# Even and odd tokens as the two streams of every product, and prompt attention over eight key blocks per head

## The chip, the core and the metric

The kernel runs on one core of a Trainium2 chip. Five engines work side by side: TensorE (PE; its weight loads are listed apart as PEld), VectorE (DVE), ScalarE (ACT), GpSimd (POOL) and SyncE (SP), which here only issues transfers. Each engine takes its instructions in the order that the scheduler wrote, and waits for others through semaphores. The metric is device microseconds of one execution, median of several; less is better.

## What is computed

One layer of a decoder, for a prompt of 256 tokens and for 8 sequences of 4 new tokens each (288 tokens in all), with 2048 features. Cut to what matters:

```python
z = x @ w_in                                  # h, gate_b, gate_c, q, k, v, g_a, g_b
ya = gate_b * causal_conv3(gate_c * h)
for g, (window, dil) in enumerate(((128, 1), (512, 4), (2048, 16))):   # 4 heads of 128 each
    # key s is allowed for query t if (t - s) % dil == 0 and 0 <= t - s <= 128 * dil
    score[g] = q[g] @ k[g].T / sqrt(128) - slope * (t - s)
yb = merge over g of softmax(score[g]) @ v[g]  # weights: the softmax denominators
x1 = LN1(ALPHA * x + (sigmoid(g_a) * (ya @ w_a) + sigmoid(g_b) * (yb @ w_b)) @ w_out)
a, b = x1 @ w_up
y = LN2(ALPHA * x1 + (silu(causal_conv3(a)) * b) @ w_down)
```

The new tokens attend to caches of keys and values; the caches are copied to outputs too. Merging the groups by their denominators is one softmax over the keys of all three groups.

## The kernel before

Everything is held by feature: 128 features on the partitions, tokens along the free dimension. The unit of work is a **product** (lines 186 to 212): one block of 128 output features for all 288 tokens. Its weight block of up to 16 x 128 x 128 comes by one transfer of up to 1 MB on SP's queue (`prepare`, three buffers "wst"), and is split into a rounded part and a rest ("whi" on ScalarE, "wlo" on VectorE, line 136 on, in half blocks, four buffers each). The activations are split the same way (`split`, line 213). `mms` then runs three matmuls for each of the 16 blocks of features, lines 208 to 210: high by high, low weight or low activation by high.

The moving operand of a matmul is read from two streams. The free dimension of x is stored as [2, 144 or more], "h" and "a", and the matmul takes column (a, h): one element of the first half, one of the second. PSUM tiles ("acc", five buffers) are [a, h]. Before, stream 0 holds tokens 0 to 143 and stream 1 tokens 144 to 287, so SBUF is in the order of the tokens and PSUM interleaves them; `h2`, `h3`, `pieces` and `from_psum` are the views that undo this.

`prompt_attention(j, ...)` (line 320) is a generator that is stepped by the products, so that its rows of matmuls stand between them; `in_a_row` keeps a row together, behind the last product matmul. For each of four heads j it takes all three groups at once. Two blocks of 128 queries (qb) see one and two blocks of 128 keys: scores (line 326), addition of the distance penalty from a table m_dist (line 332), softmax (337 to 341), transposes of V (346) and of the probabilities (354), and the value matmuls (362). A group's 128-key block is a unit here: three for the first query block, six for the second, nine for a head. Keys that the dilation rules out are in the table with a distance of 1e30. The PSUM tiles of this part are "att" (two buffers) and some of "acc".

`sample_steps` (line 407) is a second generator for the new tokens: matmuls against cache tiles, each of them 32 columns of the array wide (lines 421 and 474, PSUM tile "long", one buffer), and two small rows for the new keys and values (lines 438 and 485).

After attention come the mixer products with the convolution (`conv_in`, `conv`, `gated`, lines 524 to 563), the output products with the first norm, and the feed-forward part in three thirds of 16, 16 and 12 blocks: up products in pairs with convolution and gate, then 16 down products. In the first third the norm is applied to the products' results (`normed`, line 731), and the normed x is split for the later thirds in the down loop (line 781). In the last third the subtraction of a mean estimate n2.c (line 785, GpSimd) and the sums of the second norm (`Norm.add`, lines 639 and 640, GpSimd) run along. `finish_out` (line 671) ends the kernel: norm, gain and bias (lines 706 and 708), and six output transfers.

The tile framework's scheduler simulates the engines and orders each engine's instructions by it; `behind(i, after)` (line 118) pins one instruction behind another, without a wait.

## Time and profile before

| what | us |
|---|---|
| median of 3 runs (lowest, highest) | 1762.09 (1761.49, 1762.12) |
| profiled execution | 1763.11 |
| its span | 1761.3 |
| VectorE busy in it | 1008.2 |
| ScalarE busy in it | 798.4 |
| GpSimd busy in it | 254.8 |

How to read the profile's lines. A row of the timeline has the start and duration in us, the engine, the line of the kernel, the operation, output and inputs, the shapes, and how many instructions are merged (x10: ten of them in that stretch). A bracket gives the idle time of the engine before it and what ended that. A row of a grouped view ends with busy us, mean ns of one, and idle time before. A row of a view by stretches gives the stretch, its length, busy us with the number of instructions for PE, PEld, DVE, ACT and POOL, the granted clock, the DMA share and GB/s. Matmuls overlap in the array, so their spacing, not their duration, is what one costs. A matmul on 32-bit operands (not split) shows as two records.

### The profile page before, as it was taken

The numbers are of one execution on the slowest core, as the hardware profiler recorded it, in microseconds if no ns is written. First come the engines' busy times: TensorE is split into PE (matmuls) and PEld (weight loads), VectorE is DVE, ScalarE is ACT, GpSimd is POOL, SyncE is SP. The second block draws the span as 40 slices with busy tenths as digits, with TensorE's granted clock in tenths as the row PEclk, the third lists the DMA queues.
The fourth block names the chain that finished last, engine by engine and source line by source line (L and its number), as shares of the span: only waits on it lengthen the run. The fifth ranks groups of instructions, "written<-read, shape, count | busy, mean of one in ns | idle before, by whom it ended". The sixth has DMA issues, their size and how long they took to land.

```text
span 1761.3 us, 33600 instructions
## 1 busy us (share of the span) xinstructions
PE 1743.9 (99%) x14269; PEld 1714.4 (97%) x14269; DVE 1008.2 (57%) x1322; ACT 798.4 (45%) x1174; POOL 254.8 (14%) x403
## 2 busy tenths in 40 slices
PE   9999999999999999999999999999999999999996
PEld 9999999999999999999999999999999999999996
DVE  5444455545555444455588888774555554555554
ACT  5444444333434333344445656553454443345444
POOL 0000000000000000001155233310011110011174
PEclk9999999999999999999999999999999999999998
DMA  8477787787787887466766566656565656666662
GB/s 325 173 288 264 271 299 297 265 324 297 271 333 285 304 312 269 150 241 252 269 259 220 210 241 226 229 219 236 219 236 219 236 217 238 217 238 217 223 212 105
DMA packets 60919, 436.25 MB, mean 248 GB/s; under 512 B 7265, under 2 KB 8929, under 8 KB 16865
## 3 DMA queue, kind: packets, MB, share of 16 engines
q1 hardware_dynamic: 59040, 429.40, 65.9%
q10 hardware_dynamic: 1728, 4.72, 0.7%
q8 instruction: 111, 1.82, 0.4%
q14 instruction: 40, 0.32, 0.0%
HBM read 389.89 MB, written 94.53 MB: 275 GB/s over the span
## 4 chain that ended last, share of the span: by engine, by line
PE 96%; POOL 1%; ACT 1%; DVE 1%; issue 0%; DMA 0%; ACTq 0%; DVEq 0%
PE acc L208 31%; PE acc L210 31%; PE acc L209 31%; PE acc L276 1%; PE long L421 1%; PE long L474 1%; POOL dd L785 1%; PE att L362 0%; PE att L326 0%; ACT whi L138 0%; POOL qk_s L549 0%; ACT xh L214 0%; ACT yah L708 0%; DVE dd L684 0%; DMA yah<-in_x 0%
## 5 line engine op out<-in xcount | busy, mean ns | idle before, releaser
L139 DVE TENSOR_TENSOR wlo<-wst,whi 128x1024 fp32r<-128x1024 f32 (+1 forms) x578 | 706.9, 1224 | 617.3 <-ACT whi L138 613.2
L138 ACT CAST whi<-wst 128x1024 fp32r<-128x1024 f32 (+1 forms) x578 | 590.0, 1022 | 871.2 <-PE acc L209 767.7
L208 PE MATMUL acc<-xh,whi 128*128 128x288 f32 (+1 forms) x3216 | 923.0, 287 | 0.0
L210 PE MATMUL acc<-xh,wlo 128*128 128x288 f32 (+1 forms) x3216 | 920.5, 286 | 0.0
L209 PE MATMUL acc<-xl,whi 128*128 128x288 f32 (+1 forms) x3216 | 920.4, 286 | 0.0
L208 PEld LDWEIGHTS acc<-xh,whi 128*128 128x128 f32 x3216 | 607.8, 189 | 7.9 <-ACT h L569 2.5
L210 PEld LDWEIGHTS acc<-xh,wlo 128*128 128x128 f32 x3216 | 607.8, 189 | 0.8 <-issue 0.8
L209 PEld LDWEIGHTS acc<-xl,whi 128*128 128x128 f32 x3216 | 607.9, 189 | 0.3 <-issue 0.2
L208 PE MATMUL acc<-yah,whi 128*128 128x288 f32 x1216 | 348.0, 286 | 0.3 <-ACT yah L214 0.3
L210 PE MATMUL acc<-yah,wlo 128*128 128x288 f32 x1216 | 347.7, 286 | 0.6 <-DVE wlo L139 0.6
L209 PE MATMUL acc<-yal,whi 128*128 128x288 f32 x1216 | 347.6, 286 | 0.0
L208 PEld LDWEIGHTS acc<-yah,whi 128*128 128x128 f32 x1216 | 229.7, 189 | 3.1 <-ACT h L591 2.5
L210 PEld LDWEIGHTS acc<-yah,wlo 128*128 128x128 f32 x1216 | 229.8, 189 | 0.8 <-DVE wlo L139 0.8
L209 PEld LDWEIGHTS acc<-yal,whi 128*128 128x128 f32 x1216 | 229.8, 189 | 0.0
L549 POOL COPY qk_s<-u 128x2 f32<-128x2 f32 x44 | 41.5, 943 | 565.7 <-ACT u L758 441.1
L535 DVE SCALAR_TENSOR_TENSOR cy<-u,prm,cy 128x304 f32<-128x304 f32 x120 | 71.1, 593 | 3.4 <-ACT cy L533 0.7
L606 POOL TENSOR_TENSOR ya<-ya,dd 128x288 f32<-128x288 f32 x16 | 13.6, 851 | 306.0 <-DVE ya L605 306.0
L560 DVE TENSOR_TENSOR ya<-cy,acc 128x144 f32<-128x144 f32 x132 | 25.6, 250 | 33.6 <-PE acc L210 33.6
L549 POOL COPY cm<-u 128x2 f32<-128x2 f32 x16 | 3.0, 185 | 254.3 <-DVE u L574 254.3
L214 ACT CAST yah<-ya 128x288 fp32r<-128x288 f32 x76 | 32.7, 430 | 13.8 <-POOL ya L606 8.3
L214 DVE TENSOR_TENSOR yal<-ya,yah 128x288 fp32r<-128x288 f32 x76 | 34.9, 460 | 1.3 <-ACT yah L214 1.2
L639 POOL TENSOR_TENSOR cache<-cache,dd 128x288 f32<-128x288 f32 x29 | 28.0, 964 | 49.0 <-DVE dd L724 33.5
(179 smaller groups left out, 852.8 us busy)
## 6 DMA issues: line engine op xcount, KB each, us to landing
wst<-in_w_in SPq DMA_DIRECT2D x113, 1024.0 KB, 6.0
wst<-in_w_up SPq DMA_DIRECT2D x88, 1024.0 KB, 4.8
wst<-in_w_down SPq DMA_DIRECT2D x32, 1024.0 KB, 4.8
cache<-in_ck SPq DMA_DIRECT2D x18, 1024.0 KB, 6.4
out_o_ck<-cache SPq DMA_DIRECT2D x18, 1024.0 KB, 9.1
cache<-in_cv SPq DMA_DIRECT2D x18, 1024.0 KB, 6.3
out_o_cv<-cache SPq DMA_DIRECT2D x18, 1024.0 KB, 9.8
wst<-in_w_a SPq DMA_DIRECT2D x16, 1024.0 KB, 4.8
```

Of the source, the lines that this page charges most:

```text
L138: act.copy(hi[:, :n, :], st[:, k0 : k0 + n, :])
L139: dve.tensor_tensor(lo[:, :n, :], st[:, k0 : k0 + n, :], f32(hi[:, :n, :]), ALU.subtract)
L208: pe.matmul(out, hi[:, c, :], xh_k, start=k == 0, stop=False)
L209: pe.matmul(out, hi[:, c, :], xl_k, start=False, stop=False)
L210: last_mm[0] = pe.matmul(out, lo[:, c, :], xh_k, start=False, stop=k == nk - 1)
L214: return act.copy(hi, src), dve.tensor_tensor(lo, src, f32(hi), ALU.subtract)
L276: i = pe.matmul(o[b], first_w(term == 2, b, k), xk, start=k == 0 and term == 0, stop=k == KD - 1 and term == 2)
L421: row.append(pe.matmul(p[j * NS : (j + 1) * NS], qm[:, j, b, :], c[:, o + j * cols : o + (j + 1) * cols], start=b == 0, stop=b == NB - 1,))
L535: dve.scalar_tensor_tensor(y, u[:, i : i + YW], prm[:, w0 + i : w0 + i + 1], y, ALU.mult, ALU.add)
L549: pool.tensor_copy(dst[:, 0:2], u[:, SEQ : SEQ + 2])
L560: dve.tensor_tensor(a, b, c, ALU.mult)
L639: pool.tensor_tensor(self.s1, self.s1, d, ALU.add)
```

## The change

The two streams of a product are now the even and the odd tokens: stream h, column a is token 2a + h. PSUM is then in the order of the tokens, and SBUF tiles by feature hold evens first and odds behind, except K, V, the convolution's input and the final y, which are stored in the order of the tokens. The views change with it: x is split from a stepped view at the start, convolution input and gates go by `of_tokens` and `of_halves`, and y is written with a step of two.

In prompt attention the two query blocks are the even and the odd queries. In the groups with dilation 4 and 16 an even query sees even keys only, and an odd query odd keys, so one block of 128 keys (taken with a step of two) is enough for each; the group with dilation 1 needs both blocks of 128 keys for either. That makes four blocks for each of the two, eight for a head. The table m_dist is loaded by parity of the rows, with four transfers and a memset; the transposed probabilities go to two "acc" tiles of 512 columns.

Further, the two small rows of the new tokens are attached to the last row of their group (the first of them with an "att" tile in place of "long"). In the first third's down loop the split of the normed x is pinned behind the last gated split and the latest weight split; in the last third the subtraction of n2.c for block i is pinned behind the sums of block i - 3.

```diff
+MW = (2 + NG - 1) * P
...
+    def t2(ap):
+
+        return ap.rearrange("p (a h) -> p h a", h=2)
...
+    w_split = []
+
     def half_block(st, k0, n):
         hi = sb(wp, [P, HK, P], "whi", F32R, bufs=4)
         lo = sb(wp, [P, HK, P], "wlo", F32R, bufs=4)
-        act.copy(hi[:, :n, :], st[:, k0 : k0 + n, :])
-        dve.tensor_tensor(lo[:, :n, :], st[:, k0 : k0 + n, :], f32(hi[:, :n, :]), ALU.subtract)
+        w_split[:] = split(hi[:, :n, :], lo[:, :n, :], st[:, k0 : k0 + n, :])
         return hi, lo, n
...
     for k0, n, _ in FIRST:
         k = slice(k0, k0 + n)
-        splits.append(split(xh[:, k, :, :H], xl[:, k, :, :H], h3(xs[:, k])))
+        splits.append(split(xh[:, k, :, :H], xl[:, k, :, :H], xs[:, k].rearrange("p k (a h) -> p k h a", h=2)))
...
-    m_dist = pa[:, : C_W - C_M0]
-    pa_at = [C_W - C_M0]
+
+    m_dist = pa[:, : 2 * NG * SEQ].rearrange("p (h g k) -> p h g k", h=2, g=NG)
+    pa_at = [2 * NG * SEQ]
...
-    s_two = [pa_take(NG * 2 * P) for _ in range(2)]
+    s_two = [pa_take(MW) for _ in range(2)]
...
-    sT_flat = [xs_flat[:, NH * NG * T + c * NG * P : NH * NG * T + (c + 1) * NG * P] for c in range(3)]
-    sT_three = [t.rearrange("p (g q) -> p g q", g=NG) for t in sT_flat]
+    sT_two = [xs_flat[:, NH * NG * T + c * MW : NH * NG * T + (c + 1) * MW] for c in range(2)]
...
+    def load_distances():
+
+        pool.memset(m_dist[: P // 2, :, :, P:], BIG)
+        m0, m1 = (
+            ins["cst"][:, c : c + NG * n * P].rearrange("(a h) (g k) -> h a g k", h=2, g=NG)
+            for n, c in ((1, C_M0), (2, C_M1))
+        )
+        for h in range(2):
+            behind(sp.dma_start(m_dist[: P // 2, h, :, :P], m0[h]), w_load[0])
+            behind(sp.dma_start(m_dist[P // 2 :, h], m1[h]), w_load[0])
...
     def prompt_attention(j, qT, kT, vT):
 
-        blocks = [(qb, g, P * (qb + 1)) for qb in range(2) for g in range(NG)]
-        s3 = att(NG * P), att(2 * 2 * P), sb(ps, [P, 2 * P], "acc")
-        p_at = [(s3[0], g * P) for g in range(NG)] + [(s3[1], 0), (s3[1], 2 * P), (s3[2], 0)]
-        in_a_row([last_mm[0]] + [
-            pe.matmul(t[:, c : c + nk], qT[:, g, qb * P : (qb + 1) * P], kT[:, g, :nk], start=True, stop=True)
-            for (t, c), (qb, g, nk) in zip(p_at, blocks)
-        ])
-        s = [s_two[qb][:, : NG * P * (qb + 1)].rearrange("p (g k) -> p g k", g=NG) for qb in range(2)]
-        for (t, c), (qb, g, nk) in zip(p_at, blocks):
-            c0 = qb * NG * P + g * nk
-            dve.scalar_tensor_tensor(
-                s[qb][:, g, :], m_dist[:, c0 : c0 + nk], -SLOPE[g][j] / SCALE, t[:, c : c + nk], ALU.mult, ALU.add
-            )
+
+        q4 = h3(qT)[:, :, :, :P]
+        k4, v4 = (t[:, :, :SEQ].rearrange("p g (a h) -> p g h a", h=2) for t in (kT, vT))
+        s3 = [att(MW) for _ in range(2)]
+        row = [last_mm[0]]
+        for qb in range(2):
+            row += [
+                pe.matmul(s3[qb][:, : 2 * P], q4[:, 0, qb], kT[:, 0, :SEQ], start=True, stop=True)
+            ] + [
+                pe.matmul(s3[qb][:, (1 + g) * P : (2 + g) * P], q4[:, g, qb], k4[:, g, qb], start=True, stop=True)
+                for g in range(1, NG)
+            ]
+        in_a_row(row)
+        s = s_two
+        for qb in range(2):
+            for g in range(NG):
+                c, n = (0, 2 * P) if g == 0 else ((1 + g) * P, P)
+                m = m_dist[:, qb, g] if g == 0 else t2(m_dist[:, qb, g])[:, qb]
+                dve.scalar_tensor_tensor(
+                    s[qb][:, c : c + n], m, -SLOPE[g][j] / SCALE, s3[qb][:, c : c + n], ALU.mult, ALU.add
+                )
...
         pv = [att(NG * P) for _ in range(2)]
         row = [last_mm[0]] + [
-            pe.transpose(pv[kb][:, g * P : (g + 1) * P], vT[:, g, kb * P : (kb + 1) * P], ident)
+            pe.transpose(
+                pv[kb][:, g * P : (g + 1) * P], vT[:, 0, kb * P : (kb + 1) * P] if g == 0 else v4[:, g, kb], ident
+            )
             for kb in range(2) for g in range(NG)
         ]
         for kb in range(2):
             act.copy(v[:, kb], pv[kb].rearrange("p (g d) -> p g d", g=NG))
-        pairs = ((0, 0), (1, 0), (1, 1))
-        pt = [att(NG * P), att(NG * P), sb(ps, [P, NG * P], "acc")]
+        pt = [sb(ps, [P, MW], "acc") for _ in range(2)]
         in_a_row(row + [
-            pe.transpose(t[:, g * P : (g + 1) * P], s[qb][:, g, kb * P : (kb + 1) * P], ident)
-            for t, (qb, kb) in zip(pt, pairs) for g in range(NG)
+            pe.transpose(pt[qb][:, c * P : (c + 1) * P], s[qb][:, c * P : (c + 1) * P], ident)
+            for qb in range(2) for c in range(MW // P)
         ])
-        for sT, t in zip(sT_three, pt):
-            act.copy(sT, t.rearrange("p (g q) -> p g q", g=NG))
+        for sT, t in zip(sT_two, pt):
+            act.copy(sT, t)
...
         po = att(2 * P)
         in_a_row([last_mm[0]] + [
             pe.matmul(
-                po[:, qb * P : (qb + 1) * P], v[:, kb, g], sT[:, g],
-                start=kb == 0 and g == 0, stop=kb == qb and g == NG - 1,
+                po[:, qb * P : (qb + 1) * P], v[:, c if c < 2 else qb, max(0, c - 1)], sT_two[qb][:, c * P : (c + 1) * P],
+                start=c == 0, stop=c == MW // P - 1,
             )
-            for sT, (qb, kb) in zip(sT_three, pairs) for g in range(NG)
+            for qb in range(2) for c in range(MW // P)
         ])
         act.copy(oT, po)
-        split(ybh[:, j, :SEQ], ybl[:, j, :SEQ], oT)
+        split(h2(ybh[:, j])[:, :, :P], h2(ybl[:, j])[:, :, :P], oT.rearrange("p (h a) -> p h a", h=2))
...
+                if g == NG - 1 and b == NB - 1:
+
+                    pn = att(NG * NS)
+                    row += [
+                        pe.matmul(
+                            pn[j * NS : (j + 1) * NS, k * NS : (k + 1) * NS], q_s[:, k, j, :], k_s[:, k, j, :],
+                            start=True, stop=True,
+                        )
+                        for k in range(NG) for j in range(NH)
+                    ]
...
-        pn = sb(ps, [P, NG * NS], "long", bufs=1)
-        for j in range(NH):
-            for g in range(NG):
-                pe.matmul(
-                    pn[j * NS : (j + 1) * NS, g * NS : (g + 1) * NS], q_s[:, g, j, :], k_s[:, g, j, :],
-                    start=True, stop=True,
-                )
...
+                if g == 0 and b == NB - 1:
+
+                    row += [
+                        pe.matmul(
+                            p[j * NS : (j + 1) * NS], sTn[:, j * NS : (j + 1) * NS], vn[:, j, :], start=False, stop=True
+                        )
+                        for j in range(NH)
+                    ]
...
-                for j in range(NH):
-                    pe.matmul(
-                        p[j * NS : (j + 1) * NS], sTn[:, j * NS : (j + 1) * NS], vn[:, j, :], start=False, stop=True
-                    )
...
-            if j == 1:
-                dst, src = ((cst, ins["cst"][:, :C_M0]), (m_dist, ins["cst"][:, C_M0:]), (prm, ins["prm"]))[g]
-                behind(sp.dma_start(dst, src), w_load[0])
-        pool.tensor_copy(q_s[:, :, j, :], q_all[:, j, :, SEQ:])
+            if j == 1 and g == 1:
+                load_distances()
+            elif j == 1:
+                behind(sp.dma_start(*((prm, ins["prm"]) if g else (cst, ins["cst"][:, :C_M0]))), w_load[0])
+        pool.tensor_copy(q_s[:, :, j, :].rearrange("p g (a h) -> p g h a", h=2), h3(q_all[:, j])[:, :, :, P:])
     steps_on[0] = True
     for j in range(NH):
         kT, vT = (kv[:, j % 2, c] for c in range(2))
         for g in range(NG):
             for t in (kT, vT):
-                act.copy(h2(t[:, g, :]), product(x))
+                act.copy(t[:, g, :].rearrange("p (a h) -> p a h", h=2), product(x).rearrange("p h a -> p a h"))
...
-    def samples(t):
-        return t[:, SEQ:].rearrange("p (b r) -> p b r", b=NB)
-
-    def pieces(up, us):
-
-        return up[:, :H], up[:, H:SEQ], us
-
-    def from_psum(o):
-        return o[:, 0], o[:, 1, : SEQ - H], o[:, 1, SEQ - H :].rearrange("p (b r) -> p b r", b=NB)
+    def of_tokens(p, s):
+
+        return t2(p), s.rearrange("p b (r h) -> p h b r", h=2)
+
+    def of_halves(t):
+
+        return t[:, :, :P], t[:, :, P:].rearrange("p h (b r) -> p h b r", b=NB)
 
     def last_rows(dst, u):
         pool.tensor_copy(dst[:, 0:2], u[:, SEQ : SEQ + 2])
@@ -555,12 +590,14 @@
     def gated(out, y, o, add=None):
 
         yt = y[:, SEQ : SEQ + NB * (NT + 2)].rearrange("p (b r) -> p b r", b=NB)
-        if add is None:
-            for a, b, c in zip(pieces(out, samples(out)), pieces(y, yt[:, :, 2:]), from_psum(o)):
+        for a, b, c in zip(of_halves(h2(out)), of_tokens(y[:, :SEQ], yt[:, :, 2:]), of_halves(o)):
+            if add is None:
                 dve.tensor_tensor(a, b, c, ALU.mult)
-        else:
-            for a, b, c in ((out[:, :SEQ], y[:, :SEQ], o[:, :SEQ]), (samples(out), yt[:, :, 2:], samples(o))):
+            elif len(a.shape) == 3:
                 dve.scalar_tensor_tensor(a, c, add, b, ALU.add, ALU.mult)
+            else:
+                for h in range(2):
+                    dve.scalar_tensor_tensor(a[:, h], c[:, h], add, b[:, h], ALU.add, ALU.mult)
...
-                            dve.tensor_scalar(y[:, i], dd[:, i], self.at(self.g, i), self.at(self.b, i), ALU.mult, ALU.add)
+                            dve.tensor_scalar(t2(y[:, i]), h2(dd[:, i]), self.at(self.g, i), self.at(self.b, i), ALU.mult, ALU.add)
                     else:
-                        act.activation(y[:, i], dd[:, i], AF.Identity, bias=self.at(self.b, i), scale=self.at(self.g, i))
+                        act.activation(t2(y[:, i]), h2(dd[:, i]), AF.Identity, bias=self.at(self.b, i), scale=self.at(self.g, i))
...
                 pa, b1 = normed(pa)
-                act.activation(up, pa[:, :SEQ], AF.Identity, bias=b1)
-                act.activation(us, samples(pa), AF.Identity, bias=b1)
+                for a, b in zip(of_tokens(up, us), of_halves(pa)):
+                    act.activation(a, b, AF.Identity, bias=b1)
             else:
-                for a, b in zip(pieces(up, us), from_psum(pa)):
+                for a, b in zip(of_tokens(up, us), of_halves(pa)):
                     act.copy(a, b)
...
-            split(gh[:, k], gl[:, k], gf)
+            last_split = split(gh[:, k], gl[:, k], gf)
...
             if part == 0:
-                split(x[0][:, i], x[1][:, i], h2(dd[:, i]))
+                for i_x, *before in zip(split(x[0][:, i], x[1][:, i], h2(dd[:, i])), last_split, w_split):
+                    for b in before:
+                        behind(i_x, b)
                 dve.scalar_tensor_tensor(h2(dd[:, i]), h2(dd[:, i]), ALPHA, o, ALU.mult, ALU.add)
             else:
                 if f == KF and i > 0:
-                    pool.tensor_tensor(dd[:, i], dd[:, i], n2.c, ALU.subtract)
+                    i_c = pool.tensor_tensor(dd[:, i], dd[:, i], n2.c, ALU.subtract)
+                    if i > 2:
+                        behind(i_c, sums[i - 3])
                 dve.tensor_tensor(h2(dd[:, i]), h2(dd[:, i]), o, ALU.add)
             if f == KF:
                 if i == 0:
                     n2.first()
-                n2.add(i)
+                sums.append(n2.add(i))
```

More of the change, by code (lines that the diff above doesn't have):

```diff
@@ L320, in prompt_attention @@
     def prompt_attention(j, qT, kT, vT):
[L322 to L334 removed]
+        q4 = h3(qT)[:, :, :, :P]
[18 more added lines that the diff above has]
+                )
         for qb in range(2):
             st = sb(wk, [P, 4], "st", bufs=4)
[L337 removed]
+            dve.reduce_max(st[:, 0:1], s[qb], AX.X)
             dve.tensor_scalar_mul(st[:, 1:2], st[:, 0:1], -SCALE)
@@ L494, in sample_steps @@
         act.copy(oT, po)
-        split(ybh[:, :, SEQ:], ybl[:, :, SEQ:], oT.rearrange("p (j r) -> p j r", j=NH))
+        split(*(h3(t)[:, :, :, P:] for t in (ybh, ybl)), oT.rearrange("p (j a h) -> p j h a", j=NH, h=2))
         yield
@@ L572, in layer_kernel @@
         up, us = conv_in(u[:, :UW], R_SM + i * 2 * NB)
-        for a, b, c in zip(pieces(up, us), pieces(h, samples(h)), from_psum(pc)):
+        for a, b, c in zip(of_tokens(up, us), of_halves(h2(h)), of_halves(pc)):
             dve.tensor_tensor(a, b, c, ALU.mult)
@@ L635, in add @@
             act.activation(q, d, AF.Square)
+            i_sum = None
             if i == 0:
-                pool.tensor_copy(self.s1, d)
+                i_sum = pool.tensor_copy(self.s1, d)
             elif not last or not self.tail:
                 pool.tensor_tensor(self.s1, self.s1, d, ALU.add)
-                pool.tensor_tensor(self.s2, self.s2, q, ALU.add)
+                i_sum = pool.tensor_tensor(self.s2, self.s2, q, ALU.add)
             if i == KD - 2:
@@ L654, in add @@
                         pe.matmul((self.p1, self.p2)[k % 2], ones_d, w[:, k], start=k < 2, stop=k >= 2)
+            return i_sum
         def at(self, c, i):
@@ L738, in normed @@
         dve.scalar_tensor_tensor(t, n1.nmr, w[:, 0:1], t, ALU.mult, ALU.add)
-        return t, w[:, 1:2]
+        return h2(t), w[:, 1:2]
     cf = sb(big, [P, KF, 2 + 2 * NB], "qk_s")
@@ L744, in layer_kernel @@
     n2 = Norm(R_LN + 2 * KD, R_LN + 3 * KD, True)
+    sums = []
     for part, nf in enumerate(THIRDS):
```

1 line of the change is left out of this document (removed).

## The prediction

> **What bounds the kernel now.** I read the page first: the engines' busy time and the chain that ended last.
>
> ```profile
> span 1761.3 us, 33600 instructions
> PE 1743.9 (99%) x14269; PEld 1714.4 (97%) x14269; DVE 1008.2 (57%) x1322; ACT 798.4 (45%) x1174; POOL 254.8 (14%) x403
> PE 96%; POOL 1%; ACT 1%; DVE 1%; issue 0%; DMA 0%; ACTq 0%; DVEq 0%
> ```
>
> TensorE is busy for 1743.9 of 1761.3 us and carries 96% of the chain. So only three things can move the end: fewer or shorter TensorE instructions, the few gaps between them, and the two ends of the span where TensorE does not run. Everything that the other engines gain or lose counts only if it reaches one of these. The second view is what TensorE waited for, in us, times and longest.
>
> ```profile
> PE acc L226 <- DVE cy L223: 1.2, 1, 1.2
> PE acc L210 <- DVE wlo L139: 0.6, 1, 0.6
> PE acc L208 <- ACT yah L214: 0.3, 1, 0.3
> PE acc L276 <- ACT yal L214: 0.2, 1, 0.2
> ```
>
> That is 2.3 us in all, 1.4 of it at the start. The idle time of 17.4 us is therefore mostly the tail, about 15 us after the last matmul. The third view gives busy time in two stretches: the first third of the up-projection, the densest for VectorE, and the later feed-forward work.
>
> ```profile
> 900.00:1100.00 200.00, 200.00 (x1627) 200.00 (x1626) 163.60 (x206) 114.28 (x187) 83.18 (x100) 1.00 0.63 229
> 1500.00:1700.00 200.00, 200.00 (x1635) 200.00 (x1634) 112.27 (x154) 91.58 (x148) 36.13 (x62) 1.00 0.63 229
> ```
>
> From the second row, 200 us over 1635 matmuls, one product matmul takes 0.1223 us; two of them are 0.245 us. In the first row VectorE (third figure) is busy 163.6 of 200 us, ScalarE 114.3, GpSimd 83.2. Even there TensorE is never short of work.
>
> **The products.** Each product issues the same matmuls, with the same operand shapes: a column still takes one element of the first stored half and one of the second. Only the token that stands there differs. Main cost: nothing added, nothing removed.
>
> **Prompt attention, scores.** Before, a head has three 128-wide and three 256-wide score matmuls; after, four 128-wide and two 256-wide. Each shows as two records.
>
> ```profile
> 114.36 0.29 PE L210 MATMUL acc<-xh,wlo 128*128 128x288 f32 x1
> 114.48 1.70 PE L326 MATMUL att<-dd,yah 128*128 128x128 f32 x10
> 116.02 0.59 PE L326 MATMUL acc<-dd,yah 128*128 128x256 f32 x2
> 116.57 0.29 PE L209 MATMUL acc<-xl,whi 128*128 128x288 f32 x1
> ```
>
> From the last product matmul before the row to the second one behind it, 116.57 - 114.36 = 2.21 us; less two product matmuls, the 12 records cost 1.965 us. The row of value matmuls of the same head gives the price of a narrow record:
>
> ```profile
> 138.12 0.29 PE L210 MATMUL acc<-xh,wlo 128*128 128x288 f32 x1
> 138.24 2.17 PE L362 MATMUL att<-yah,yal 128*128 128x128 f32 x18
> 140.37 0.29 PE L209 MATMUL acc<-xl,whi 128*128 128x288 f32 x1
> ```
>
> 140.37 - 138.12 - 0.245 = 2.005 us over 18 records, 0.1114 each. Six narrow score records are then 0.668 us, and a wide one is (1.965 - 0.668)/6 = 0.216. After: 8 x 0.1114 + 4 x 0.216 = 1.755 us, so 0.21 less for a head, **0.84** for four.
>
> **Value matmuls.** Nine per head become eight: two records less, 4 x 2 x 0.1114 = **0.89** us.
>
> **Transposes of the probabilities.** Nine per head become eight.
>
> ```profile
> 174.22 0.64 PEld L354 LDWEIGHTS att<-cst,yal 128*128 128x128 f32 x6 [0.84 <-ACT yal L350]
> ```
>
> Six loads in 0.64 us, 0.107 each; four fewer are **0.42** us. The six transposes of V stay. Attention saves 2.15 us together.
>
> The unknown here is the operand step. For the second and third head group the keys are now read with a step of two elements (16 matmuls, 32 records), and V for its transposes too. The trace before has no such step on TensorE. Its nearest rows are the product matmuls, whose columns alternate between two places 640 or 576 bytes apart and still take only 0.1223 us for 288 columns. From below the cost is nothing; from above I double a narrow record, 32 x 0.1114 = 3.6 us. I take nothing, as the nearest row jumps further and pays nothing.
>
> The Trainium skill (SBUF — State Buffer, "Door 1: The DMA port swizzle", note on cachelines) says that an access which crosses to a new 16-byte line pays unless two accesses hit the line. A step of two fp32 elements has exactly two hits, so by the rule the step is free and the sum is unchanged; but the products, with one hit on each line in turn, should by the same rule run slow, and the rows above do not bear that out.
>
> **Places of the rows.** The transposed probabilities now use two accumulator buffers, not two attention buffers and an accumulator, so they no longer wait for V's copies. In the first head that wait let sample work in between:
>
> ```profile
> 130.82 0.31 PEld L354 LDWEIGHTS att<-cst,yal 128*128 128x128 f32 x3 [0.20 <-issue]
> 131.30 0.15 PEld L421 LDWEIGHTS long<-cache,sw 128*32 128x32 f32 x6 [0.17 <-issue]
> ```
>
> Each change between the two shapes cost 0.17 to 0.20 us of weight-load idle; two of them may go. I take 0.2 us (bounds 0 and 0.4). The two small sample rows (new keys' scores, new values) are attached to the last row of their group, where before they broke into a product:
>
> ```profile
> 443.73 0.29 PE L210 MATMUL acc<-xh,wlo 128*128 128x288 f32 x1
> 443.94 0.65 PE L438 MATMUL long<-qk_s 128*32 128x32 f32 x24
> 444.74 0.29 PE L209 MATMUL acc<-xl,whi 128*128 128x288 f32 x1
> ```
>
> 444.74 - 443.73 - 0.245 = 0.77 us, of which the 24 records, issued over about 0.46 us, remain; 0.25 to 0.3 us is the break. I take 0.25 for each of the two rows, **0.5** us (bounds 0 and 0.6). The new keys' scores move from the single "long" buffer to an attention buffer, so they need not wait for VectorE to empty the former; prompt attention, whose second head stands at 174 us, has released its buffers by 443.
>
> **The two gaps in the middle.** The first lies at the end of the first third:
>
> ```profile
> 1166.81 0.29 PE L209 MATMUL acc<-yal,whi 128*128 128x288 f32 x1
> 1167.44 0.51 PE L208 MATMUL acc<-yah,whi 128*128 128x288 f32 x2 [0.34 <-ACT yah L214]
> ```
>
> 1167.44 - 1166.81 - 0.122 = 0.51 us. Behind it:
>
> ```profile
> 1155.23 4.42 POOL L549 COPY qk_s<-u 128x2 f32<-128x2 f32 x1 [9.71 <-ACT u L754]
> ```
>
> ```profile
> 1155.44 3.03 DVE L214 TENSOR_TENSOR xl<-dd,xh 128x288 fp32r<-128x288 f32 x8
> ```
>
> Eight VectorE splits of the next x in a row, drawn ahead of the last gated block, held a two-element GpSimd copy for 4.42 us, and the block's chain came late. The change puts each of those splits behind the last gated split and behind the latest weight split. The 16 pairs then stand in the down products, where both engines idle at each weight split. The second gap:
>
> ```profile
> 1703.74 0.29 PE L209 MATMUL acc<-yal,whi 128*128 128x288 f32 x1
> 1704.62 0.39 PE L210 MATMUL acc<-yah,wlo 128*128 128x288 f32 x1 [0.60 <-DVE wlo L139]
> ```
>
> 1704.62 - 1703.74 - 0.122 = 0.76 us. Its cause:
>
> ```profile
> 1681.88 15.96 POOL L785 TENSOR_TENSOR dd<-dd,cache 128x288 f32<-128x288 f32 x14 [13.56 <-ACT cache L628]
> ```
>
> ```profile
> 1699.75 0.44 ACT L635 ACTIVATE cy<-dd 128x288 f32<-128x288 f32 x1 [4.25 <-POOL cache L640]
> ```
>
> ```profile
> 1702.67 1.90 DVE L139 TENSOR_TENSOR wlo<-wst,whi 128x1024 fp32r<-128x1024 f32 x1 [5.48 <-ACT whi L138]
> ```
>
> Fourteen GpSimd subtractions issued in a row delayed the sums, ScalarE waited 4.25 us for a buffer, its weight cast came late and VectorE's with it. The change holds subtraction i behind sum i - 3. I count both gaps as gone: **1.27** us. What is late next is the same chain with a shorter head; TensorE already waits for nothing else there.
>
> **Other engines.** Convolution input and gate go from three instructions (144, 112, 32 wide) to two (256, 32) in mixer and later thirds, which saves fixed cost off the path. In the first third the gate goes from two instructions to three, about 0.2 us for each of 16 blocks, against 36 us of VectorE slack in 200: hidden. Should it not be hidden it is 3 us. PSUM rows read with a step of two cost nothing on ScalarE, as these two copies show, the first stepped and the second not:
>
> ```profile
> L515 ACT COPY dd<-acc 128x288 f32<-128x288 f32 x24 | 9.4, 392 | 0.0
> L628 ACT COPY cache<-att 128x288 f32<-128x288 f32 x2 | 0.8, 395 | 0.3 <-PE att L627 0.3
> ```
>
> 392 against 395 ns. A step of two in SBUF I have only by that neighbour. The distance table takes four transfers instead of one, plus a memset on GpSimd: about three more issues on SP's queue, some 1.5 us, ahead of the next weight load on the same queue. Three weight buffers and a split block stand ahead of TensorE, each a product long (48 x 0.1223 = 5.9 us). Hidden; if the cover fails, 1 to 2 us.
>
> **The ends.** At the start x is split from a stepped view:
>
> ```profile
> 4.87 0.67 ACT L214 CAST xh<-yah 128x576 fp32r<-128x576 f32 x1 [0.94 <-DMA yah<-in_x]
> 6.12 0.85 PE L276 MATMUL acc<-xh,yal 128*128 128x288 f32 x2 [0.21 <-ACT yal L214]
> ```
>
> TensorE starts on the first casts. If a stepped read costs twice, the first x cast adds 0.67 us and VectorE's split as much: 0 to 1.3 us. I take 0.1. In the tail, ScalarE and VectorE now write y with a step:
>
> ```profile
> 1752.32 4.77 ACT L708 ACTIVATE yah<-dd,prm 128x288 f32<-128x288 f32 x9 [0.39 <-DVE dd L684]
> 1754.98 1.44 DVE L706 TENSOR_SCALAR yah<-dd,prm 128x288 f32<-128x288 f32 x4
> ```
>
> Nine ScalarE rows end at 1757.09, four VectorE rows at 1756.42, and output transfers follow. Bounds: nothing, or a doubling, +4.8 us on ScalarE. I take 0.3 us.
>
> **Sum.** -0.84 - 0.89 - 0.42 - 0.2 - 0.5 - 1.27 + 0.1 + 0.3 = -3.7 us. The profiled execution took 1763.11 us with its span of 1761.3 (1.8 around it), 1.0 above the median of 1762.09. So a span of about 1757.6, an execution of 1759.4, and a median of **1758.4 us**, 0.21% faster. A difference of 0.2% (3.5 us) is about what a measurement of this kernel can tell from no change, so the sum sits on that line.
>
> **Rivals.** First, *new gaps take part of it back*. The scheduler orders every engine anew, and the first third has VectorE at 82% with an instruction added in each block. For it: two such gaps of 0.5 and 0.8 us stand in the kernel before, both from other engines' order. Against it: the change pins the orders behind exactly these. If the two gaps stay or two others of 0.5 to 0.8 come, and the row breaks bring nothing, the sum is -3.7 + 1.27 + 0.7 = -1.7: 1760.4 us, within 0.2%.
>
> Second, *the step of two costs double wherever it stands on the path*: 3.6 us in attention's score records, 4.8 in the tail's ScalarE rows, 1.3 at the start, 9.7 together. Then +6.0 us, **1768.1 us**, slower. It decides from +7.2 us, so it needs attention and most of the tail. For it: no row shows a stepped SBUF access on these engines. Against it: stepped PSUM reads at 392 ns and the alternating product operand.
>
> Third, *the change does less than it says*: attention's 2.15 us only. That comes if TensorE's gaps and breaks are set by something else: 1760.3 us with the ends as taken, again within 0.2%.
>
> **Chances.** Forecast 0.50 (faster by over 0.2%), first and third rivals together 0.36 (within), second 0.14 (slower). Range: below, everything open comes free (-0.4 at the ends), the row breaks come at their upper bounds (-0.3), and each of eight other sample rows loses a break of 0.25 us too (2.0), 1755.6 with rounding; above, the second rival with half its price, 1763.3, and a little more for its upper part: 1755.6 to 1765.
>
> **What would show it.** Right: the score, value and transpose rows shorter by 0.21, 0.22 and 0.1 us a head, with a narrow stepped record at 0.11; no TensorE wait above 0.3 us near the end of the first third and in the last 60 us; y's ScalarE rows still 0.53 us apart. Wrong: stepped records at 0.2, ScalarE's tail rows near 1 us, a later first matmul, or new waits of TensorE for a weight split. A time above 1763 would say that a stall was made, not that the savings are missing.

## The result, and the profile after

The changed kernel takes 1757.22 us (median of 10 runs, 1756.95 to 1758.0) against 1761.66 (10 runs, 1761.42 to 1762.37): 4.4 us less, ratio 0.9975 with a 95% interval of 0.9967 to 0.9982. The prediction was 1758.4, 3.7 us less. The page of the changed kernel:

```profile
span 1756.2 us, 33518 instructions
PE 1738.8 (99%) x14257; PEld 1710.7 (97%) x14257; DVE 1006.7 (57%) x1278; ACT 797.9 (45%) x1142; POOL 243.7 (14%) x404
...
PE 99%; DMA 0%; DVE 0%; ACT 0%; SPq 0%; ACTq 0%; issue 0%; DVEq 0%
```

TensorE now carries 99% of the chain, against 96%. What TensorE waited for in the changed kernel:

```profile
PE acc L235 <- DVE cy L232: 1.2, 1, 1.2
PE acc L285 <- ACT yal L223: 0.7, 2, 0.4
PE acc L285 <- ACT whi L223: 0.3, 1, 0.3
```

Only waits at the start are left; the two gaps of the middle (0.6 on a weight split and 0.3 on a gated split) are gone. The two stretches shown of before:

```profile
900.00:1100.00 200.00, 200.00 (x1627) 200.00 (x1626) 165.10 (x217) 113.31 (x186) 79.41 (x98) 1.00 0.63 226
1500.00:1700.00 200.00, 200.00 (x1635) 200.00 (x1634) 113.53 (x144) 94.33 (x140) 36.92 (x63) 1.00 0.64 229
```

The first third is not lighter for VectorE (163.6 before), and the pace of a product matmul is the same, 200 us over 1635. So the gain is not in the products. It is in the rows between them and in the two gaps. The first head's scores, from the last product matmul to the second one behind the row:

```profile
113.72 0.29 PE L219 MATMUL acc<-xh,wlo 128*128 128x288 f32 x1
113.84 0.59 PE L349 MATMUL att<-dd,yah 128*128 128x256 f32 x2
114.28 0.62 PE L351 MATMUL att<-dd,yah 128*128 128x128 f32 x4
...
115.74 0.29 PE L218 MATMUL acc<-xl,whi 128*128 128x288 f32 x1
```

115.74 - 113.72 - 0.245 = 1.775 us, against 1.965 before: 0.19 less. The four narrow records read keys with a step of two, and stand (0.62 - 0.276)/3 = 0.115 us apart. The value row:

```profile
134.71 0.29 PE L219 MATMUL acc<-xh,wlo 128*128 128x288 f32 x1
134.83 1.95 PE L391 MATMUL att<-yah,yal 128*128 128x128 f32 x16
...
136.74 0.29 PE L218 MATMUL acc<-xl,whi 128*128 128x288 f32 x1
```

136.74 - 134.71 - 0.245 = 1.785 us, 0.22 less than 2.005. V's and the probabilities' transposes now stand in one block:

```profile
127.25 0.29 PE L219 MATMUL acc<-xh,wlo 128*128 128x288 f32 x1
127.27 0.78 PEld L374 LDWEIGHTS att<-cst,dd 128*128 128x128 f32 x6
127.38 0.86 PE L374 MATMUL att<-cst,dd 128*128 128x128 f32 x6
128.07 1.04 PE L383 MATMUL acc<-cst,yal 128*128 128x128 f32 x8
...
129.07 0.29 PE L218 MATMUL acc<-xl,whi 128*128 128x288 f32 x1
```

129.07 - 127.25 - 0.245 = 1.575 us for all fourteen, with no wait for V's copies. The row of sample work that stood among them in the first head before has moved to 142 us, where it costs 2.08 us by itself. Before, both together took 4.15 us (128.09 to 132.48, less two product matmuls), so the first head's transposes gain 0.50 us. In the other heads there is next to nothing to gain; the second one, before and after:

```profile
171.49 0.29 PE L210 MATMUL acc<-xh,wlo 128*128 128x288 f32 x1
...
175.38 0.29 PE L209 MATMUL acc<-xl,whi 128*128 128x288 f32 x1
```

```profile
169.75 0.29 PE L219 MATMUL acc<-xh,wlo 128*128 128x288 f32 x1
...
171.56 0.29 PE L218 MATMUL acc<-xl,whi 128*128 128x288 f32 x1
```

175.38 - 171.49 - 0.245 = 3.645 us before, with a sample row of 2.05 among it, so 1.595; 171.56 - 169.75 - 0.245 = 1.565 after: 0.03 less. Further on, a sample row by itself, and the last one of the keys, which now has the new keys' scores behind it:

```profile
346.50 0.29 PE L219 MATMUL acc<-xh,wlo 128*128 128x288 f32 x1
346.71 1.92 PE L450 MATMUL long<-cache,sw 128*32 128x512 f32 x16
...
348.79 0.29 PE L218 MATMUL acc<-xl,whi 128*128 128x288 f32 x1
```

```profile
409.40 0.29 PE L219 MATMUL acc<-xh,wlo 128*128 128x288 f32 x1
409.62 1.92 PE L450 MATMUL long<-cache,sw 128*32 128x512 f32 x16
411.36 0.37 PE L458 MATMUL att<-qk_s 128*32 128x32 f32 x24
...
411.88 0.29 PE L218 MATMUL acc<-xl,whi 128*128 128x288 f32 x1
```

Alone, a row costs 348.79 - 346.50 - 0.245 = 2.05 us; with the new keys' scores 411.88 - 409.40 - 0.245 = 2.24. They cost 0.19 us, against 0.77 where they broke into a product. GpSimd's two-element copy near the end of the first third, 4.42 us before:

```profile
1149.44 0.79 POOL L584 COPY qk_s<-u 128x2 f32<-128x2 f32 x1 [7.69 <-ACT u L795]
```

The tail rows of y, now written with a step of two (ScalarE's):

```profile
1747.04 4.83 ACT L747 ACTIVATE yah<-dd,prm 128x288 f32<-128x288 f32 x9 [0.35 <-DVE dd L723]
```

4.83 us for nine against 4.77.

**The start must be taken out before profiles are compared.** The spans differ by 5.1 us, 0.7 more than the medians. In the profiled execution of before, TensorE ran the first product matmuls at half pace until 10.7 us (the first row: two of them in 0.69 us, 0.24 apart; the second, at full pace: two in 0.41, 0.12 apart):

```profile
7.33 0.69 PE L276 MATMUL acc<-xh,yal 128*128 128x288 f32 x2
...
10.85 0.41 PE L276 MATMUL acc<-xh,yal 128*128 128x288 f32 x2
```

In the changed kernel full pace was there with the first product matmuls, at 6.35 us: the first two took 0.51 us behind a wait, where the profiled execution of before took 0.85 at 6.12. Its first x cast took 0.72 us where before it took 0.67:

```profile
5.05 0.72 ACT L223 CAST xh<-yah 128x576 fp32r<-128x576 f32 x1 [1.12 <-DMA yah<-in_x]
...
6.35 0.51 PE L285 MATMUL acc<-xh,yal 128*128 128x288 f32 x2 [0.44 <-ACT yal L223]
```

So I measure from the last of the first three products (last start of their low-weight records) to the norm's matmuls behind the last product. The view of one line has the first and the last start. Before:

```profile
L276 PE MATMUL acc<-xh,wlo x16: 286/286/447, 10.0 to 26.2; 128*128 128x288 f32 x16
```

```profile
L648 PE MATMUL att<-cache,ones_d x4: 406/406/406, 1744.2 to 1744.9; 128*128 128x288 f32 x4
```

1744.2 - 26.2 = 1718.0 us. After:

```profile
L285 PE MATMUL acc<-xh,wlo x16: 286/286/286, 8.7 to 25.5; 128*128 128x288 f32 x16
```

```profile
L686 PE MATMUL att<-cache,ones_d x4: 406/406/406, 1738.9 to 1739.6; 128*128 128x288 f32 x4
```

1738.9 - 25.5 = 1713.4 us, 4.6 us less. The tail behind it is 1761.3 - 1744.2 = 17.1 us before and 1756.2 - 1738.9 = 17.3 after.

### The profile page after: what moved, and what is told of

The parts are those of the page before. It is cut to its first block, busy times and chain, and to the rows that moved or that the text cites. A ratio compares the mean times of both kernels' runs of the same rounds, so it can differ in the third digit from the quotient of the medians.

```text
span 1756.2 us, 33518 instructions
## 1 busy us (share of the span) xinstructions
PE 1738.8 (99%) x14257; PEld 1710.7 (97%) x14257; DVE 1006.7 (57%) x1278; ACT 797.9 (45%) x1142; POOL 243.7 (14%) x404
## 4 chain that ended last, share of the span: by engine, by line
PE 99%; DMA 0%; DVE 0%; ACT 0%; SPq 0%; ACTq 0%; issue 0%; DVEq 0%
PE acc L217 32%; PE acc L219 31%; PE acc L218 31%; PE long L506 1%; PE long L450 1%; PE acc L285 1%; DMA dd<-in_w_in 0%; PE att L391 0%; ACT yah L747 0%; DVE dd L723 0%; PE att L351 0%; PE acc L383 0%; PE att L349 0%; PE att L374 0%; PE att L687 0%; PE att L686 0%
## 5 line engine op out<-in xcount | busy, mean ns | idle before, releaser
L223 DVE TENSOR_TENSOR wlo<-wst,whi 128x1024 fp32r<-128x1024 f32 (+2 forms) x584 | 709.1, 1215 | 613.1 <-ACT whi L223 607.6
L223 ACT CAST whi<-wst 128x1024 fp32r<-128x1024 f32 (+2 forms) x584 | 593.3, 1017 | 888.0 <-PE acc L218 777.7
L595 DVE TENSOR_TENSOR ya<-cy,acc 128x256 f32<-128x256 f32 x88 | 23.5, 310 | 33.8 <-PE acc L219 33.7
```

Of the source, the lines that this page charges most:

```text
L223: return act.copy(hi, src), dve.tensor_tensor(lo, src, f32(hi), ALU.subtract)
L595: dve.tensor_tensor(a, b, c, ALU.mult)
```

## The experiments

Theory A: the gain is the sum of three named parts on TensorE (attention's records, the two pins, the two attached rows). Rival B: it comes from the order that the scheduler drew anew. Rival C: the step of two costs something that hides in the sum. Theory S: the start is luck of one execution. Theory K: it belongs to the kernel. They were timed in three groups, each beside the kernel before on one chip; "before" in the table is its median in the same group, and "stretch" is the length defined above, here from starts that the timeline gives to 0.01 us. With these, the stretch of before is 1718.01 us and that of the changed kernel 1713.38.

| kernel | median us | before | ratio (95%) | first products end | stretch |
|---|---|---|---|---|---|
| before_pins | 1760.76 | 1761.68 | 0.9993 (0.9984 to 1.0002) | 25.5 | 1716.53 |
| before_rows | 1761.38 | 1761.68 | 0.9998 (0.9989 to 1.0007) | 25.3 | 1717.11 |
| before_pins_rows | 1759.77 | 1761.68 | 0.9988 (0.9979 to 0.9997) | 25.0 | 1715.61 |
| after_rows_apart | 1758.69 | 1761.68 | 0.9982 (0.9973 to 0.9991) | 24.8 | 1714.30 |
| after_no_x_pin | 1758.13 | 1761.51 | 0.998 (0.9971 to 0.9989) | 25.1 | 1714.02 |
| after_no_sum_pin | 1758.0 | 1761.51 | 0.9981 (0.9973 to 0.999) | 25.4 | 1714.25 |
| after_flat_keys | 1756.9 | 1761.51 | 0.9974 (0.9963 to 0.9985) | 24.7 | 1713.16 |
| after_flat_ends | 1756.99 | 1761.51 | 0.9975 (0.9965 to 0.9985) | 24.8 | 1713.38 |
| before_again | 1761.74 | 1761.99 | 0.9998 (0.9989 to 1.0007) | 25.1 | 1718.03 |
| before_rows_again | 1760.72 | 1761.99 | 0.9994 (0.9985 to 1.0002) | 25.3 | 1717.11 |
| after_again | 1757.24 | 1761.99 | 0.9974 (0.9963 to 0.9984) | 24.6 | 1713.38 |
| after_warm22 | 1757.63 | 1761.99 | 0.9975 (0.9965 to 0.9985) | 24.7 | 1713.38 |

The intervals are about as wide as the parts, so a single ratio does not tell them apart. The stretches do: three kernels that were profiled twice repeat them to 0.02 us.

**The pins alone.** The kernel before, with:

```diff
-                split(x[0][:, i], x[1][:, i], h2(dd[:, i]))
+                for i_x, *before in zip(split(x[0][:, i], x[1][:, i], h2(dd[:, i])), last_split, w_split):
+                    for b in before:
+                        behind(i_x, b)
...
-                    pool.tensor_tensor(dd[:, i], dd[:, i], n2.c, ALU.subtract)
+                    i_c = pool.tensor_tensor(dd[:, i], dd[:, i], n2.c, ALU.subtract)
+                    if i > 2:
+                        behind(i_c, sums[i - 3])
```

> The kernel before with the two pins alone (x split behind the last gated split and the latest weight split; subtraction i behind sums i - 3). Theory A, the gain is a sum of named parts: both TensorE gaps (0.51 and 0.76 us) go, 1.3 us faster than the kernel before, and no TensorE wait is left between 1100 and 1740 us. Rival B, the gain comes from the order that the scheduler drew anew: the pins alone bring 0 to 0.3 us, or another gap of the same size opens.

TensorE's waits in it:

```profile
PE acc L277 <- ACT yal L215: 1.3, 2, 1.0
PE acc L227 <- DVE cy L224: 1.2, 1, 1.2
PE acc L277 <- ACT whi L215: 0.2, 1, 0.2
```

Both gaps are gone, no other has come, and the stretch is 1.5 us shorter (1718.0 to 1716.5). Theory A holds and rival B falls for this part. The median gained 0.9.

**The rows alone.** The kernel before, with the blocks of the change that attach the new keys' scores and the new values to their groups' last rows.

```diff
+                if g == NG - 1 and b == NB - 1:
+
+                    pn = att(NG * NS)
...
+                if g == 0 and b == NB - 1:
+
+                    row += [
```

> The kernel before with the two small rows of the new tokens attached to their groups' last rows, alone. Theory A: 0.9 us faster than before, as the profiles of before and after differ by that between 414 and 699 us. By the prediction's term: 0.5 us. Rival B: within 0.3 us of before.

The stretch is 0.9 us shorter, as theory A says, but the median only 0.3. The run was made again (below).

**Pins and rows together**, both edits in the kernel before.

> The kernel before with pins and rows, so without the even and odd streams and with nine blocks per head. Theory A: the two add up, 2.2 us faster than before, and what is left to the changed kernel (2.2 us) is attention. Rival B: not the sum of the two runs beside it by more than 0.5 us.

The stretch is 2.4 us shorter, against 1.5 + 0.9 = 2.4 for the two apart: they add up. The median gained 1.9, which is more than the 0.9 + 0.3 of the two medians beside it. From here to the changed kernel the stretch loses 1715.6 - 1713.4 = 2.2 us: the even and odd streams with eight blocks, which no run takes apart, as the blocks need the streams. The rows of the four heads account for all of it (see below).

**The rows taken out of the changed kernel.**

```diff
-                if g == NG - 1 and b == NB - 1:
-
-                    pn = att(NG * NS)
...
+        pn = sb(ps, [P, NG * NS], "long", bufs=1)
```

> The changed kernel with the two small rows apart again, as they were before. Theory A: 0.9 us slower than the changed kernel (3.5 us faster than before). Rival B: within 0.3 us of the changed kernel.

Stretch +0.9 us, median +1.5. The part is worth the same in both kernels.

**Each pin taken out of the changed kernel.** First the x split's:

```diff
-                for i_x, *before in zip(split(x[0][:, i], x[1][:, i], h2(dd[:, i])), last_split, w_split):
-                    for b in before:
-                        behind(i_x, b)
+                split(x[0][:, i], x[1][:, i], h2(dd[:, i]))
```

> The changed kernel without the pin on the x split. Theory A: a TensorE gap of about 0.5 us at the end of the first third comes back, 0.5 us slower than the changed kernel (3.9 us faster than before). Rival: the new copies and gates of the first third had removed that gap by themselves, and nothing changes.

A TensorE row with a wait at the end of the first third is back, in the place and size of before:

```profile
1163.27 0.51 PE L217 MATMUL acc<-yah,whi 128*128 128x288 f32 x2 [0.37 <-ACT yah L223]
```

Stretch +0.65 us, and GpSimd's two-element copy takes 4.39 us again. Then the subtractions':

```diff
-                    if i > 2:
-                        behind(i_c, sums[i - 3])
```

> The changed kernel without the pin on the subtractions. Theory A: GpSimd issues the subtractions in one row again and a TensorE gap of about 0.8 us comes back near 1700 us, 0.8 us slower than the changed kernel (3.6 us faster than before). Rival: the new order does not need the pin, and nothing changes.

TensorE's wait on the weight split, and GpSimd's fourteen subtractions in a row, both as before:

```profile
PE acc L219 <- DVE wlo L223: 0.6, 1, 0.6
```

```profile
1677.32 15.96 POOL L827 TENSOR_TENSOR dd<-dd,cache 128x288 f32<-128x288 f32 x14 [13.54 <-ACT cache L665]
```

Stretch +0.87 us. The two together are 1.5, what the pins brought to the kernel before. The new copies and gates had not removed either gap by themselves.

**Keys and V without a step.**

```diff
-        k4, v4 = (t[:, :, :SEQ].rearrange("p g (a h) -> p g h a", h=2) for t in (kT, vT))
+        k4, v4 = (t[:, :, :SEQ].rearrange("p g (h a) -> p g h a", h=2) for t in (kT, vT))
```

> The changed kernel with K and V of the second and third group read without a step (first and second 128 tokens in place of the even and odd ones, so the prompt's attention is that of other keys). Theory A, a step of two is free on TensorE: within 0.2 us of the changed kernel, narrow score records at 0.11 us in both. Rival C, the step costs: faster by up to 3.5 us at double price; the transposes of V, 0.86 us for six against 0.82 before, would by themselves give 0.2 us.

The first head's first narrow records, and the weight loads of its V transposes, now without a step:

```profile
113.43 0.61 PE L351 MATMUL att<-dd,yah 128*128 128x128 f32 x4
...
126.40 0.69 PEld L374 LDWEIGHTS att<-cst,dd 128*128 128x128 f32 x6
```

Four narrow records take 0.61 us, against 0.62 with the step; six weight loads 0.69, against 0.78. In the trace of the changed kernel the four stepped loads among the six took 0.195 to 0.211 us each and the two others 0.138 to 0.152; without the step all took 0.140 to 0.142. Most of that is hidden beside the matmuls: a head's score row is 0.02 us shorter and its row of transposes 0.04, and the stretch 0.22 over four heads. So the step costs about 0.2 us in all, a sixteenth of the 3.6 that doubling it would be. Theory A's "within 0.2" was just missed, rival C's price falls.

**The ends without a step.** x split from two halves of the tokens, y written as it lies.

```diff
-        splits.append(split(xh[:, k, :, :H], xl[:, k, :, :H], xs[:, k].rearrange("p k (a h) -> p k h a", h=2)))
+        splits.append(split(xh[:, k, :, :H], xl[:, k, :, :H], h3(xs[:, k])))
...
-                        act.activation(t2(y[:, i]), h2(dd[:, i]), AF.Identity, bias=self.at(self.b, i), scale=self.at(self.g, i))
+                        act.activation(y[:, i], dd[:, i], AF.Identity, bias=self.at(self.b, i), scale=self.at(self.g, i))
```

> The changed kernel with x split and y written without a step at the two ends (so the tokens stand in another order in the streams and in y). Theory A: ScalarE's x casts return from 0.72 and 1.30 to 0.67 and 1.15 us and its tail rows from 4.83 to 4.77 us for nine; 0 to 0.2 us faster than the changed kernel. Rival C, the step costs at the ends: 0.5 us faster or more.

ScalarE's x casts at the start, and its tail rows:

```profile
5.02 0.67 ACT L223 CAST xh<-yah 128x576 fp32r<-128x576 f32 x1 [0.99 <-DMA yah<-in_x]
...
12.65 1.15 ACT L223 CAST xh<-yah 128x1152 fp32r<-128x1152 f32 x1 [0.28 <-DMA yah<-in_x]
```

```profile
1746.32 4.78 ACT L747 ACTIVATE yah<-dd,prm 128x288 f32<-128x288 f32 x9 [0.39 <-DVE dd L723]
```

Both returned to the durations of before. The first products ended at 24.8 us and the median of 1756.99 us lies 0.2 under the changed kernel's 1757.22, inside the spread of either's runs; nothing at the ends costs the changed kernel more than that.

**The start.** Three kernels unchanged a second time, on one chip.

> The kernel before, unchanged, for a second profile of it. Theory S, the start is luck of one execution: full matmul pace comes near 6 to 7.5 us and the first three products end at 24.6 to 25.5 us, not at 26.2; from there to the last products 1718.0 us again, within 0.2; span 1759.8 to 1760.7. Rival K, the start belongs to the kernel: 26.2 us and a span of 1761.3 again.

```profile
L276 PE MATMUL acc<-xh,wlo x16: 286/286/286, 8.5 to 25.1; 128*128 128x288 f32 x16
```

```profile
L648 PE MATMUL att<-cache,ones_d x4: 406/406/406, 1743.1 to 1743.8; 128*128 128x288 f32 x4
```

And its first product matmuls, at full pace:

```profile
6.10 0.51 PE L276 MATMUL acc<-xh,yal 128*128 128x288 f32 x2 [0.51 <-ACT yal L214]
```

The trace's record of the granted clock has full clock from 5.1 us here, before the first product and even earlier than theory S expected; it has it from 10.8 us in the first execution. The first products ended at 25.1 us and the stretch is 1743.1 - 25.1 = 1718.0 again; the span is 1760.3 where it was 1761.3. Theory S holds.

The clock is not all of this luck. In the other thirteen traces full clock begins at 4.1 to 7.0 us and the first products end at 24.6 to 25.5 us, and the one does not order the other: the earliest clock, in after_no_sum_pin, goes with 25.4.

> The kernel before with the attached rows, unchanged, a second time. Its median was 0.3 us under that of before where its trace behind the start was 0.9 us shorter. Theory S: the 0.6 us is luck of the start, and the median now lies 0.6 to 1.2 us under before_again. Rival K: 0.3 us again, with first products that end later than those of before.

1.0 us under before_again, in the range of theory S, so the 0.3 of the first time was not the rows' price; the stretch is 1717.1 us both times. What made it 0.3 is not shown: the profiled first products ended at 25.3 us both times, 0.2 later than before_again's, so the single number of rival K came too. Medians of one program lie apart by as much, 1761.74 and 1761.99 for the kernel before in this group.

> The changed kernel, unchanged, a second time: beside before_again on one chip. Theory A and S: first products to last products 1713.4 us within 0.2, median 4.3 to 4.7 us under before_again.

```profile
L285 PE MATMUL acc<-xh,wlo x16: 286/286/286, 8.1 to 24.6; 128*128 128x288 f32 x16
```

```profile
L686 PE MATMUL att<-cache,ones_d x4: 406/406/406, 1738.0 to 1738.7; 128*128 128x288 f32 x4
```

1738.0 - 24.6 = 1713.4 us, and the median is 4.5 us under before_again. The first products end 0.9 us earlier than in the changed kernel's first profile (25.5). Transfers differ there: that time ScalarE waited 1.27 us for a weight transfer before its cast at 19.76 us, this time the same cast ran at 17.80 without a wait.

The last run tried whether the start can be had for good:

```diff
-N_WARM = 18
+N_WARM = 22
```

> The changed kernel with 22 matmuls on zeros at the start in place of 18, about 0.96 us more at half pace, which would end near 6.9 us where the first casts are there at 6.0 to 6.4. Theory S, an array that is kept busy gets full pace early in every execution: first products end by 24.9 us, 0 to 0.3 us faster than after_again. Rival: transfers set the start anyway and the first matmul is only later: 0 to 0.5 us slower.

```profile
4.74 1.29 PE L235 MATMUL acc<-cy 128*128 128x288 f32 x8
6.30 0.51 PE L285 MATMUL acc<-xh,yal 128*128 128x288 f32 x2 [0.27 <-ACT yal L223]
```

The array is busy nearly until the first casts, and the first products ended at 24.7 us. That is no earlier than after_again, and the median is 0.4 us higher. The zeros ended at 6.0 us, not 6.9, as full clock began at 4.9 us within them, just as in after_again with 18; whether 22 bring it early in every execution, one profile can't show. The rival is nearer: the added matmuls gain nothing, and that transfers set the end is its likely cause, not shown by this run. No kernel tried that computes the layer beats the changed one.

## Why the prediction came out as it did

**Attention (-2.15, and -0.2 for the first head's order): right in sum, in part by luck.** The stretch gives -2.2 for streams and blocks together, and the rows of the four heads add up to the same 2.23: 0.76 in the scores (forecast 0.84), 0.89 in the values (0.89), 0.58 in the transposes (0.42, and 0.2 for the order). The last two terms were each off and made up for one another. In the second to fourth head the transposes are 0.03 us shorter, not the 0.1 that the prediction named as a sign of being right; the first head gains 0.50, where 0.1 and 0.2 were forecast. Of the 0.08 us that are missing in each of these heads, V's stepped weight loads are about half, which I left unpriced; the rest is open. The bound of 3.6 us for the step of two was rightly left near its lower end; the step measured about 0.2. This trace has 0.115 against 0.111 us for a narrow record with and without the step. The Trainium skill's rule (SBUF — State Buffer, "Door 1: The DMA port swizzle"), by which two hits in a line of 16 bytes are free, agrees with that nearly; the stepped weight loads, at about 0.20 against 0.14 us, do not bear it out.

**The two gaps (-1.27): right.** -1.5 by the pins alone, 0.65 and 0.87 by each. The mechanism was shown from both sides, with the pins put into the kernel before and taken out of the changed one.

**The attached rows (-0.5): right in mechanism, too small.** -0.9 measured: the new keys' scores fell from 0.77 to 0.19 us, the new values from 0.55 to 0.22. The term that was mis-sized most is the price of the new keys' records, which I left at 0.46 us and only saved the break. The change also issues them with the head as the inner loop, so that successive records go to different strips of 32 columns: 24 records are then (0.37 - 0.196)/23 = 7.6 ns apart, where (0.65 - 0.196)/23 = 19.7 ns stood before (0.196 us is one record). The Trainium skill (TensorE: Matmul & The Clock Gate, "Part 3: Packing small matmuls — row/col tiling") says that matmuls on different tiles of the array overlap; the trace agrees. In the row before, the records of one strip stand 32 ns apart and those of the next strip start beside them; after, the four strips run together, each with a record about every 30 ns. No run changed the loop order alone. I read the diff for the place of the row and not for its loop order.

**The start (+0.1): wrong as read, harmless.** The stepped cast of x does cost, 1.30 against 1.15 us for 1152 elements, but the first products end no later for it (25.5 and 24.6 us with it, 24.8 without). The first product matmul starts at 6.35 and 6.18 us, against 6.12 and 6.10 before; that was named as a sign of being wrong, but before_rows_again, without the step, has 6.46. What I had not priced is that the profiled execution of before was itself unlucky there. I put it 1.0 us above the median of three runs and carried that along; against the median of ten it is 1.45, and most of that is the late pace: its first products end 1.1 us later than before_again's.

**The tail (+0.3): small and too high.** 17.1 to 17.3 us, and 17.2 in before_again (1760.3 - 1743.1): +0.1.

**Rivals.** New gaps did not come. The step does not cost double anywhere. The change did all that it says. Since -2.2, -1.5, -0.9 and +0.1 make -4.5, within 0.1 us of the medians' difference, nothing of that size is left to the scheduler's luck.

## What to carry to other kernels

Where one engine is busy for 99% of the span, price a change by the spacing of that engine's records in the rows that it touches, their order and their breaks included, and look at each term again afterwards: here the sum came within 0.7 us while four of its terms were off by half or more. Before two profiles are compared, cut out the part that varies between executions, here the first 25 us, and measure between two landmarks that both kernels have; the stretch between them repeated to 0.02 us where medians moved by 0.6. When a list of short helpers is issued in one row ahead of work that the path waits for, pin them behind that work; two such pins were worth 1.5 us here without any instruction less.

## What the runs showed of the hardware

The time at which TensorE comes to full clock varied between executions of one program: 5.1 and 10.8 us in the kernel before, 6.3 and 4.9 in the changed one, by the traces' record of the granted clock. The Trainium skill (TensorE: Matmul & The Clock Gate, "Part 1: The HAM clock gate") has full clock granted after a busy window of about 3.4 us that runs free of the kernel's start, so that the onset varies from run to run; these traces agree, as full clock lasts 1737.384, 1740.797 or 1744.211 us in all fourteen of them, in steps of 3.413 us. Why it came as late as 10.8 us once is open. The granted clock in the profile's stretches reads 1.00 even where the spacing is double, as the record begins only with full clock.

A GpSimd copy of two elements took 4.42 us while VectorE ran eight splits back to back between two weight splits, and 0.79 us beside one weight split where the eight were pinned elsewhere. Without that pin in the changed kernel it took 4.39 us again.
